# Where the second 1/rms of the feed-forward activations is multiplied in: inside the weight loop, or behind its last weight sum

## The chip, the cores and the metric

The kernel runs on one core of one Trainium2 chip. The metric is the device time in microseconds (us). The core has five engines that run their own queues of instructions in order: TensorE (PE; its weight loads are listed as PEld), VectorE (DVE), ScalarE (ACT), GpSimd (POOL) and SyncE (SP, which here only issues DMAs). Operands lie in SBUF; matmul results are written to PSUM, in eight banks of 128 x 512 float32.

## The reference

One layer of a decoder trunk on 512 tokens of width 1024, in float32: a mixer, a memory cross-attention and a feed-forward part, each with a residual. The change lies in the last:

```python
def rms_norm(x, g):
    var = jnp.mean(xf * xf, axis=-1, keepdims=True)
    return xf * lax.rsqrt(var + EPS) * g

hf = rms_norm(x, norm_ffn[l])
gate, up = jnp.split(hf @ w_ffn_in[l], 2, axis=-1)
x = x + (jax.nn.silu(gate) * up) @ w_ffn_out[l]
return rms_norm(x, norm_final)
```

FFN_HIDDEN is 2816, that is 22 tiles of 128. The 1/rms of a token is one factor for its whole row, so `hf @ w` can be computed without it and multiplied by it afterwards: once for the gate, ahead of silu, and once for `up`.

## The kernel before

Activations are held transposed: features on the 128 partitions, the 512 tokens along the free dimension. Each float32 operand is split into a rounded part (`hi`, a copy on ACT) and the rest (`lo`, a subtraction on VectorE), and each product is three matmuls (hi x hi, hi x lo, lo x hi).

The feed-forward input product is done by tiles m = 0 to 21, each with a gate and an up column block. For a tile the two column blocks, the two token halves and the pairs of feature blocks form a 2 x 2 block product, which is computed with seven products in place of eight. `product(m, i)` (i = 0 to 6, line 660) is 12 matmuls of 256 columns; the seven need seven combinations of the weights:

- `ffn_load(m)` (lines 619 to 629) fetches them: `wg` (two blocks), `ws` (one block to two places, line 625) and `a` from the SP queue, then a DMA from POOL's queue that adds two further blocks into `ws` (line 628). The tiles `wg` and `ws` share a ring of four buffers, as do later the rows of the output weights.
- `ffn_raw` (line 638) makes the two combinations that are still lacking, i = 3 and i = 6, by an addition on POOL: the weight sums.
- `ffn_form` splits each combination: the copy on ACT (L649), the subtraction on VectorE (L650). It runs six products ahead.

Results are put together from PSUM: `reads` (copies on ACT, L680; additions on VectorE, L682 and L685), `second` (VectorE, L690, which reads a bank that TensorE then goes on to accumulate in), and `evict` in three parts: part 0 multiplies the gate by 1/rms (`r2b`, a tile of 128 x 512 with the tokens' factors in every partition; VectorE, L697), part 1 is silu (ACT, L699), part 2 multiplies silu by `up` with the sign (VectorE, L704, two halves, one from PSUM and one from the SBUF tile `sb`) into `act[m]`, and then multiplies `act[m]` by `r2b` on POOL (L706).

The order of TensorE, ACT and VectorE in this part is written out by hand (`tc.manual_schedule`): the list `uses` interleaves the products of neighbouring tiles, and eviction of tile m-2 runs beside tile m. Tiles 20 and 21 are the last; their evictions come after the last products. POOL and SP are ordered by a scheduler.

The output product follows: `act[k]` is split (L169 on ACT, L170 on VectorE), the row block k of `w_ffn_out` is loaded and split (`load_w`, L143, L150, L151), and 8 x 3 matmuls of 512 columns (`out_step`, L155 to L157) add to eight PSUM banks that the input product used before. Tiles 0 and 1 are split inside the hand-written part, so that TensorE can start on the output product between the last input products. The last four row blocks are held back for `finish`, which adds the residual and makes the final norm.

Of the kernel before, what the change touches and what calls it, by code (L numbers as in the profile page):

```python
# [11 lines left out]
ALU = mybir.AluOpType  # L12
# [26 lines left out]
def hybrid_layer(ctx: ExitStack, tc: tile.TileContext, xT_d, memT_d, cols_d, wv_d, win_d,  # L39
                 wbr_d, wmix_d, wmq_d, wmk_d, wmv_d, wmo_d, wfi_d, wfo_d, out):  # L40
    nc = tc.nc
# [15 lines left out]
    def nm(s):  # L57
        count[0] += 1
        return f"{s}{count[0]}"

    def unit(s, cols=512):
        return upool.tile([P, cols], F32R, tag="u", name=nm(s), padded_shape=[P, 512])
# [4 lines left out]
    def f(ap):  # L67
        return ap.bitcast(F32)
# [38 lines left out]
    def after(i, earlier):  # L107
        for e in earlier:
            tc.add_manual_dep(i.ins, e.ins.name, mybir.DependencyInfo(
                mybir.DependencyClass.NoSync, mybir.DependencyReason.DATA), reason="order")  # L110
# [28 lines left out]
    def load_w(src, cols=P):  # L139

        k = D // cols
        raw = wpool.tile([P, D], F32, tag="wr", name=nm("wr"))
        i = nc.sync.dma_start(raw, src)  # L143
        if count[1] < FIRST:
            count[1] += 1
            chained(i)
        hi = wpool.tile([P, k, cols], F32R, tag="wh", name=nm("wh"))
        lo = wpool.tile([P, k, cols], F32R, tag="wl", name=nm("wl"))
        h2, l2 = (t.rearrange("p k c -> p (k c)") for t in (hi, lo))
        nc.scalar.copy(h2, raw)  # L150
        nc.vector.tensor_tensor(out=l2, in0=raw, in1=f(h2), op=ALU.subtract)  # L151
        return hi, lo
# [12 lines left out]
    def split(src, s, scale=None, cols=512):  # L165

        hi, lo = unit(s + "h", cols), unit(s + "l", cols)
        if scale is None:
            casts.append(nc.scalar.copy(hi, src))  # L169
            nc.vector.tensor_tensor(out=lo, in0=src, in1=f(hi), op=ALU.subtract)  # L170
        else:
            nc.scalar.activation(hi, src, AF.Copy, scale=scale)
            nc.vector.scalar_tensor_tensor(out=lo, in0=src, scalar=scale, in1=f(hi),
                                           op0=ALU.mult, op1=ALU.subtract)
        return hi, lo
# [260 lines left out]
    for m in range(KD):  # L436
# [8 lines left out]
        w = load_w(wbr_d[m])  # L445
# [11 lines left out]
    for m in range(KD):  # L457
        w = load_w(wmk_d[m])
# [11 lines left out]
    for n in range(2):  # L470
        pss = [ztile("vm") for _ in range(MT)]
        for c in range(4):
            w = load_w(wmv_d[n, c], 512)
# [82 lines left out]
    for h in range(MH):  # L556
# [12 lines left out]
        for t2 in range(2):  # L569
# [6 lines left out]
                                           in1=r1s[:, 2 * t2:2 * t2 + 2], op0=ALU.mult,  # L576
# [10 lines left out]
            for i in range(2):  # L587
                nc.vector.tensor_scalar(out=pr[:, i * MEM:(i + 1) * MEM],
                                        in0=pr[:, i * MEM:(i + 1) * MEM],
# [10 lines left out]
        for j in range(2):  # L600
# [3 lines left out]
            for m in range(MT):  # L604
                w = vm[m][c // 512]
# [5 lines left out]


    KP = KD // 2
    AHEAD = 6
    FORM_TAGS = ((wpool, "wh"), (wpool, "wl"), (wpool, "wh"), (wpool, "wl"), (fpool, "wf"))

    raws = {}

    def ffn_load(m):

        a = wfi_d[m].rearrange("p (i c) -> p i c", i=4)
        wg = wpool.tile([P, 2, 512], F32, tag="wr", name=nm("wg"))
        nc.sync.dma_start(wg, a[:, 0:2, :])
        s13 = wpool.tile([P, 2, 512], F32, tag="wr", name=nm("ws"))
        nc.sync.dma_start(s13, a[:, 2:3, :].broadcast_to([P, 2, 512]))
        a22 = fpool.tile([P, 512], F32, tag="w2", name=nm("a22"), bufs=4)
        nc.sync.dma_start(a22, a[:, 3, :])
        nc.gpsimd.dma_start(s13, a[:, 0:4:3, :], accum_op=ALU.add)  # L628
        raws[m] = [wg[:, 0, :], wg[:, 1, :], s13[:, 1, :], None, s13[:, 0, :], a22, None]

    def ffn_raw(m, i):
        if i == 0:
            ffn_load(m)
        w = raws[m]
        if w[i] is None:
            w[i] = fpool.tile([P, 512], F32, tag="w2", name=nm("s2"), bufs=4)
            a, b = (w[2], w[0]) if i == 3 else (w[3], w[1])
            nc.gpsimd.tensor_tensor(out=w[i], in0=a, in1=b, op=ALU.add)  # L638
        return w[i]

    wforms, made = {}, [0]
# [1 line left out]
    def ffn_form(m, i):  # L643

        raw = ffn_raw(m, i)
        pool, tag = FORM_TAGS[made[0] % len(FORM_TAGS)]
        made[0] += 1
        w = pool.tile([P, 2, 512], F32R, tag=tag, name=nm("wf"))
        nc.scalar.copy(w[:, 0, :], raw)  # L649
        nc.vector.tensor_tensor(out=w[:, 1, :], in0=raw, in1=f(w[:, 0, :]), op=ALU.subtract)  # L650
        wforms[m, i] = w

    def product(ps, m, i, ks=range(KP)):

        w = wforms[m, i]
        for k in ks:
            hi, lo = (w[:, j, k * P:(k + 1) * P] for j in range(2))
            xh, xl = x2f[k][i]
            for j, (a, b) in enumerate(((hi, xh), (hi, xl), (lo, xh))):
                nc.tensor.matmul(ps[:, :HS], a, b, start=i < 3 and k == 0 and j == 0,  # L660
                                 stop=k == KP - 1 and j == 2, skip_group_check=True)

    banks, act, silus, late = {}, {}, [], []
# [11 lines left out]
    def reads(m, i):  # L675

        b = banks[m]
        z, s, t = b["z"][:, :HS], b["s"], b["t"]
        if i in (0, 3, 4):
            nc.scalar.copy((s[:, :HS], None, None, s[:, HS:], t[:, :HS])[i], z)  # L680
        elif i == 1:
            nc.vector.tensor_tensor(out=b["g"][:, :HS], in0=b["v"][:, :HS], in1=s[:, :HS],  # L682
                                    op=ALU.add)
        elif i == 6:
            nc.vector.tensor_tensor(out=b["g"][:, HS:], in0=b["y"][:, :HS], in1=s[:, HS:],  # L685
                                    op=ALU.add)
# [6 lines left out]
    def evict(m, part):  # L693
        b = banks[m]
        g = b["g"]
        if part == 0:
            nc.vector.tensor_tensor(out=g, in0=g, in1=r2b[0], op=ALU.mult)  # L697
        elif part == 1:
            silus.append(nc.scalar.activation(g, g, AF.Silu))  # L699
        else:  # L700
            a = act[m] = f(unit("act"))
            for half, u in enumerate((b["z"][:, :HS], b["t"][:, HS:])):
                sl = slice(half * HS, (half + 1) * HS)
                nc.vector.scalar_tensor_tensor(out=a[:, sl], in0=u, scalar=-1.0, in1=g[:, sl],  # L704
                                               op0=ALU.mult, op1=ALU.mult)
            nc.gpsimd.tensor_tensor(out=a, in0=a, in1=r2b[0], op=ALU.mult)  # L706

    uses = [(0, 0), (0, 1), (0, 2)]
    for m in range(NF):
# [6 lines left out]
    r2b = [None]  # L716
    for n in range(AHEAD):
        ffn_form(*uses[n])
    with tc.manual_schedule(engines={mybir.EngineType.PE, mybir.EngineType.Activation,
                                     mybir.EngineType.DVE}):  # L720
        for ks in (range(KP - 1), range(KP - 1, KP)):
            for m, i in uses[:3]:
                product(bank_of(m, i) if ks[0] == 0 else banks[m]["zvy"[i]], m, i, ks)
        for n, (m, i) in enumerate(uses):
            if n > 2:
                product(bank_of(m, i), m, i)
            if (m, i) == (1, 0):
                r2b[0] = mean2[1]("r0b", bank=mmtile)
            if i == 4:
                reads(m, i)  # L730
            elif i == 5 and m == NF - 1:
                reads(m, i)
                second(m)
            else:
                if i == 1 and m > 0:
                    second(m - 1)
                reads(m, i)
            if n + AHEAD < len(uses):
                ffn_form(*uses[n + AHEAD])

            if i == 0 and m > 1:
                evict(m - 2, 0)
            elif i == 4 and 0 < m < NF - 1:
                evict(m - 1, 1)
            elif i == 1 and m > 1:
                evict(m - 2, 2)
            if m == NF - 1 and i in (0, 1):
                actp[i] = split(act[i], "act")
            if (m, i) == (NF - 2, 6):
                evict(m, 0)  # L750
                evict(m, 1)
            if (m, i) == (NF - 1, 5):
                evict(NF - 2, 2)
# [2 lines left out]
        evict(NF - 1, 2)  # L756
    r2b = r2b[0]
    act = [act[m] for m in range(NF)]


    acc = [mmtile("f") for _ in range(2)] + [ztile("f") for _ in range(4)]
# [7 lines left out]
    act = [actp[k] if k in actp else split(a, "act") for k, a in enumerate(act)]  # L769
    for k in range(NF - HOLD):  # L770
        w = load_w(wfo_d[k], D)
# [105 lines left out]
```

## Time and profile before

| | us |
|---|---|
| median of three runs | 895.28 |
| lowest and highest | 892.0, 899.22 |
| the profiled execution, its own time | 893.23 |
| the span in it, first to last instruction | 891.3 |

The profile is of one execution. Its times are measured from the start of the span. A row of the view in time has the start, the duration, the engine, the line, the operation, the output and the inputs, and in brackets how long the engine had been idle and what ended that. A row of the waits has the waiting engine and line, what it waited for, the sum, the number of waits and the longest. A row by stretches has the length, then for PE, PEld, DVE, ACT and POOL the busy time and the number of instructions, the granted TensorE clock, the share of DMA and GB/s. An engine's busy time includes what it spends inside an instruction that is held up. "wf<-ws" is output and inputs by the program's names.

The input product of the feed-forward part runs from 524.6 to 757.8 us, the output product from 754.8 to about 870.

### The profile page before, as it was taken

To read this page: it belongs to the slowest core of one execution; us is meant where nothing else is said; L and a number is where in the kernel's file an instruction comes from. 1 tells how busy PE (TensorE), PEld (TensorE's weight loads), DVE (VectorE), ACT (ScalarE), POOL (GpSimd) and SP (SyncE) were. 2 spreads that over 40 slices of the span, in tenths; PEclk is the share of its full clock that TensorE was granted. 3 is DMA by queue.
4 is the path that set the end of the run, shared out by engine and by line. 5 is a ranking of instruction groups with operands and counts; after the bars stand their busy time and mean duration, and the time that the engine had idled before them with its cause. 6 is when DMAs were issued, how large, how long until landed. Compare 5 with 4: busy or idle time off the path is not lost. (4 is left out here: it accounts for less than half of the span.)

```text
span 891.3 us, 12942 instructions
## 1 busy us (share of the span) xinstructions
PE 868.6 (97%) x5002; PEld 758.6 (85%) x5002; DVE 629.1 (71%) x951; ACT 438.6 (49%) x799; POOL 167.2 (19%) x177
## 2 busy tenths in 40 slices
PE   7999999999999999999999999999999998999995
PEld 5878887888888899888888889999999998888894
DVE  5768788886544566555555799999999998922236
ACT  5566576565332344433444565455555545711143
POOL 0021221111000000000000214555566543100003
PEclk9999999999999999999999999999999999999998
DMA  7332212225332345423211545667676665332202
GB/s 284 119 107 83 83 60 72 71 72 177 107 107 94 107 146 187 152 95 97 70 50 45 133 102 146 170 175 192 182 193 166 172 174 173 97 95 95 71 1 95
DMA packets 41469, 107.29 MB, mean 120 GB/s; under 512 B 3760, under 2 KB 7872, under 8 KB 41408
## 3 DMA queue, kind: packets, MB, share of 16 engines
q1 hardware_dynamic: 34848, 94.39, 31.8%
q0 software_dynamic: 6016, 11.56, 8.1%
q8 instruction: 39, 0.64, 0.3%
q10 hardware_dynamic: 544, 0.52, 0.2%
q14 instruction: 22, 0.18, 0.1%
HBM read 104.36 MB, written 2.10 MB: 119 GB/s over the span
## 5 line engine op out<-in xcount | busy, mean ns | idle before, releaser
L150 ACT CAST wh<-wr 128x1024 fp32r<-128x1024 f32 x106 | 111.3, 1052 | 246.7 <-issue 84.5
L151 DVE TENSOR_TENSOR wl<-wr,wh 128x1024 fp32r<-128x1024 f32 x106 | 130.1, 1227 | 100.1 <-ACT wh L150 99.8
L155 PE MATMUL pr<-xgh,wh 128*128 128x512 f32 x288 | 112.6, 391 | 0.1
L157 PE MATMUL pr<-xgh,wl 128*128 128x512 f32 x288 | 112.3, 390 | 0.0
L156 PE MATMUL pr<-xgl,wh 128*128 128x512 f32 x288 | 112.2, 390 | 0.0
L628 POOL DMA_DIRECT2D ws<-in_w_ffn_in_dram x22 | 26.4, 1202 | 320.7 <-DVE x L519 288.3
L155 PE MATMUL f<-acth,wh 128*128 128x512 f32 (+1 forms) x208 | 74.6, 359 | 0.3 <-DVE act L704 0.3
L156 PE MATMUL f<-actl,wh 128*128 128x512 f32 (+1 forms) x208 | 74.1, 357 | 0.0
L157 PE MATMUL f<-acth,wl 128*128 128x512 f32 (+1 forms) x208 | 74.1, 358 | 0.0
L660 PE MATMUL z<-xdh,wf 128*128 128x256 f32 x352 | 70.4, 283 | 0.0
L155 PEld LDWEIGHTS pr<-xgh,wh 128*128 128x128 f32 x288 | 54.1, 188 | 11.4 <-issue 0.4
L157 PEld LDWEIGHTS pr<-xgh,wl 128*128 128x128 f32 x288 | 54.1, 188 | 11.4
L156 PEld LDWEIGHTS pr<-xgl,wh 128*128 128x128 f32 x288 | 54.1, 188 | 10.7
L660 PEld LDWEIGHTS z<-xdh,wf 128*128 128x128 f32 x352 | 58.0, 192 | 0.0
L660 PE MATMUL z<-xdl,wf 128*128 128x256 f32 x176 | 49.8, 283 | 0.0
L638 POOL TENSOR_TENSOR s<-ws,wg 128x512 f32<-128x512 f32 x22 | 33.3, 1512 | 85.3 <-DMA ws<-in_w_ffn_in_dram 35.1
L650 DVE TENSOR_TENSOR wf<-ws,wf 128x512 fp32r<-128x512 f32 x44 | 45.5, 1033 | 3.5 <-ACT wf L649 3.5
L697 DVE TENSOR_TENSOR fg<-fg,r0b 128x512 f32<-128x512 f32 x22 | 46.3, 2103 | 0.0
L155 PEld LDWEIGHTS f<-acth,wh 128*128 128x128 f32 x208 | 39.3, 189 | 6.6 <-DVE act L704 0.7
L157 PEld LDWEIGHTS f<-acth,wl 128*128 128x128 f32 x208 | 39.1, 189 | 5.7
L156 PEld LDWEIGHTS f<-actl,wh 128*128 128x128 f32 x208 | 39.3, 189 | 5.5
L706 POOL TENSOR_TENSOR act<-act,r0b 128x512 f32<-128x512 f32 x22 | 38.3, 1742 | 13.9 <-DVE act L704 13.9
(256 smaller groups left out, 2291.6 us busy)
## 6 DMA issues: line engine op xcount, KB each, us to landing
wr<-in_w_in_dram SPq DMA_DIRECT2D x36, 512.0 KB, 3.4
wg<-in_w_ffn_in_dram SPq DMA_DIRECT2D x22, 512.0 KB, 4.9
ws<-in_w_ffn_in_dram SPq DMA_DIRECT2D x22, 512.0 KB, 4.8
ws<-in_w_ffn_in_dram POOLq DMA_DIRECT2D x22, 512.0 KB, 5.7
wr<-in_w_ffn_out_dram SPq DMA_DIRECT2D x22, 512.0 KB, 3.4
a<-in_w_ffn_in_dram SPq DMA_DIRECT2D x22, 256.0 KB, 3.3
wr<-in_w_branch_dram SPq DMA_DIRECT2D x8, 512.0 KB, 3.4
wr<-in_w_mem_k_dram SPq DMA_DIRECT2D x8, 512.0 KB, 3.4
```

Source lines behind the costliest of these rows:

```text
L150: nc.scalar.copy(h2, raw)
L151: nc.vector.tensor_tensor(out=l2, in0=raw, in1=f(h2), op=ALU.subtract)
L155: nc.tensor.matmul(ps, a[0], b[0], start=start, stop=False, **kw)
L156: nc.tensor.matmul(ps, a[0], b[1], start=False, stop=False, **kw)
L157: nc.tensor.matmul(ps, a[1], b[0], start=False, stop=stop, **kw)
L628: nc.gpsimd.dma_start(s13, a[:, 0:4:3, :], accum_op=ALU.add)
L638: nc.gpsimd.tensor_tensor(out=w[i], in0=a, in1=b, op=ALU.add)
L650: nc.vector.tensor_tensor(out=w[:, 1, :], in0=raw, in1=f(w[:, 0, :]), op=ALU.subtract)
L660: nc.tensor.matmul(ps[:, :HS], a, b, start=i < 3 and k == 0 and j == 0, stop=k == KP - 1 and j == 2, skip_group_check=True)
L697: nc.vector.tensor_tensor(out=g, in0=g, in1=r2b[0], op=ALU.mult)
L706: nc.gpsimd.tensor_tensor(out=a, in0=a, in1=r2b[0], op=ALU.mult)
```

## The change

For tiles 0, 1 and 2 the multiplication of `act[m]` by `r2b` on POOL stays where it was. For tiles 3 to 21 it is taken out of `evict` and issued after the hand-written part, still on POOL, and each is ordered behind the last weight sum (`after` adds an order without a semaphore).

```diff
+    SCALED = 3
...
-    raws = {}
+    raws, sums = {}, []
...
-            nc.gpsimd.tensor_tensor(out=w[i], in0=a, in1=b, op=ALU.add)
+            sums.append(nc.gpsimd.tensor_tensor(out=w[i], in0=a, in1=b, op=ALU.add))
...
-            nc.gpsimd.tensor_tensor(out=a, in0=a, in1=r2b[0], op=ALU.mult)
+            if m < SCALED:
+                nc.gpsimd.tensor_tensor(out=a, in0=a, in1=r2b[0], op=ALU.mult)
...
     act = [act[m] for m in range(NF)]
+    for a in act[SCALED:]:
+        after(nc.gpsimd.tensor_tensor(out=a, in0=a, in1=r2b, op=ALU.mult), sums[-1:])
```

In the built program the instructions of TensorE, VectorE, ACT and SP stand in the same order as before. On POOL the nineteen multiplications now follow one another behind the two last weight sums, in the order of the tiles; in the program before, tile m's stood behind the first weight sum of tile m+2 or so and ahead of the next DMA issue of POOL.

## The prediction

> **What bounds the kernel now.** First the head of the page and its row for the instruction that moves, then the busy time by stretches.
>
> ```profile
> span 891.3 us, 12942 instructions
> ...
> PE 868.6 (97%) x5002; PEld 758.6 (85%) x5002; DVE 629.1 (71%) x951; ACT 438.6 (49%) x799; POOL 167.2 (19%) x177
> ...
> L706 POOL TENSOR_TENSOR act<-act,r0b 128x512 f32<-128x512 f32 x22 | 38.3, 1742 | 13.9 <-DVE act L704 13.9
> ```
> ```profile
> 540.00:740.00 200.00, 197.68 (x1634) 195.63 (x1633) 195.06 (x252) 106.33 (x213) 107.37 (x76) 1.00 0.67 176
> ...
> 750.40:753.80 3.40, 3.40 (x18) 3.40 (x17) 2.52 (x5) 1.32 (x2) 0.00 (x0) 0.51 0.43 136
> ...
> 780.00:860.00 80.00, 80.00 (x373) 67.06 (x372) 19.97 (x20) 16.30 (x19) 0.00 (x0) 1.00 0.22 73
> ```
>
> TensorE is the bound nearly everywhere, so only time in which it stands still can be won. The columns of the second view are PE, PEld, DVE, ACT, POOL and then the granted clock. In the input half of the feed-forward part (540 to 740) VectorE is as full as TensorE, 195 of 200 us; in the output half (780 to 860) VectorE has 20 of 80 us and POOL nothing. The change carries POOL work from the full stretch to the empty one, but what counts is the passage between, 740 to 762. Third, who TensorE waits for from 515 to 765:
>
> ```profile
> PE z L660 <- ACT sa L680: 2.8, 2, 2.1
> PE y L660 <- DVE sb L690: 1.5, 5, 0.3
> PE f L155 <- DVE act L704: 0.3, 1, 0.3
> ```
>
> Fourth, one period of the loop, in time:
>
> ```profile
> 601.74 0.39 PE L660 MATMUL y<-xoh,wf 128*128 128x256 f32 x1 [0.32 <-DVE sb L690]
> ...
> 602.67 0.38 SPq L625 DMA_DIRECT2D ws<-in_w_ffn_in_dram  x1
> ...
> 603.67 1.40 POOL L638 TENSOR_TENSOR s<-ws,wg 128x512 f32<-128x512 f32 x1 [3.48 <-DMA ws<-in_w_ffn_in_dram]
> ...
> 603.83 1.78 DVE L650 TENSOR_TENSOR wf<-a,wf 128x512 fp32r<-128x512 f32 x1
> ...
> 605.03 1.76 POOL L706 TENSOR_TENSOR act<-act,r0b 128x512 f32<-128x512 f32 x1
> ...
> 605.54 0.41 DVE L685 TENSOR_TENSOR fg<-y,sa 128x256 f32<-128x256 f32 x1
> ...
> 605.87 1.46 DVE L650 TENSOR_TENSOR wf<-ws,wf 128x512 fp32r<-128x512 f32 x1
> ...
> 607.71 1.20 POOL L628 DMA_DIRECT2D ws<-in_w_ffn_in_dram  x1 [0.92 <-ACT wf L649]
> ...
> 608.46 2.35 DVE L697 TENSOR_TENSOR fg<-fg,r0b 128x512 f32<-128x512 f32 x1
> 608.48 1.76 POOL L638 TENSOR_TENSOR s<-s,wg 128x512 f32<-128x512 f32 x1
> ...
> 612.01 0.69 DVE L650 TENSOR_TENSOR wf<-ws,wf 128x512 fp32r<-128x512 f32 x1
> ...
> 612.73 0.38 SPq L625 DMA_DIRECT2D ws<-in_w_ffn_in_dram  x1
> ```
>
> A VectorE instruction with both inputs in SBUF takes 0.69 us alone (612.01) and 1.46 to 2.35 beside a POOL instruction, and it ends about 0.55 us after POOL's: 603.67+1.40 is 605.07 and the subtraction that began at 603.83 ends at 605.61; 605.03+1.76 is 606.79 and the next ends at 607.33. They take turns. The instruction at 605.54, which reads PSUM, takes its 0.41 us in the middle of a POOL instruction. So VectorE's full load is partly waiting, and each multiplication at L706 costs it 1.46-0.69 = 0.8 us a tile.
>
> **The change, part by part.** *The loop.* A row of twelve matmuls gives TensorE's pace:
>
> ```profile
> 727.06 1.60 PE L660 MATMUL z<-xf,wf 128*128 128x256 f32 x12
> 728.50 0.28 PE L660 MATMUL z<-xch,wf 128*128 128x256 f32 x1
> ```
>
> 1.44 us for twelve, 0.120 each; 1634 of them are 196.1 us of the 200, so 3.9 are lost. Of the two waits on ACT one lies past 740 (2.1), the other (2.8-2.1 = 0.7) before it; the loop itself loses 3.2. Those are the waits on DVE sb L690: VectorE comes late. With 16 multiplications gone from inside the loop (tiles 3 to 18) VectorE has 0.8 us more in each 10.06 us (602.67 to 612.73) and comes in time. What would be late next is the ring of the weight sum: plain DMA (602.67 to 607.71, 5.04), POOL's DMA issue and sum (to 610.25, 2.54), the blocked VectorE multiplication (to 610.81), three short ones and the subtraction (to 612.70) that frees the slot for the next plain DMA. It is as long as TensorE's 84 matmuls (84 x 0.120 = 10.1), and L706 is not in it: POOL idles 0.92 before its DMA issue. But a VectorE that comes 0.8 us earlier has L697 done ahead of POOL's sum, and the ring shortens by that. I take -3.0; the bounds are 0 (ring unchanged) and -3.9.
>
> *The passage.* The rows from the last tiles on, POOL first, then VectorE:
>
> ```profile
> 741.42 3.34 POOL L638 TENSOR_TENSOR s<-s,wg 128x512 f32<-128x512 f32 x2 [1.28 <-issue]
> ...
> 757.56 1.30 POOL L706 TENSOR_TENSOR act<-act,r0b 128x512 f32<-128x512 f32 x1 [7.42 <-DVE act L704]
> ```
> ```profile
> 741.81 1.78 DVE L697 TENSOR_TENSOR fg<-fg,r0b 128x512 f32<-128x512 f32 x1
> 743.52 1.79 DVE L170 TENSOR_TENSOR actl<-act,acth 128x512 fp32r<-128x512 f32 x1
> 745.23 0.68 DVE L650 TENSOR_TENSOR wf<-s,wf 128x512 fp32r<-128x512 f32 x1
> ...
> 747.77 1.21 DVE L151 TENSOR_TENSOR wl<-wr,wh 128x1024 fp32r<-128x1024 f32 x1
> 748.90 1.78 DVE L170 TENSOR_TENSOR actl<-act,acth 128x512 fp32r<-128x512 f32 x1
> ...
> 753.30 0.42 DVE L685 TENSOR_TENSOR fg<-y,sa 128x256 f32<-128x256 f32 x1 [0.88 <-PE y L660]
> ...
> 756.66 0.42 DVE L704 SCALAR_TENSOR_TENSOR act<-z,fg 128x256 f32<-128x256 f32 x1 [0.87 <-ACT fg L699]
> ...
> 757.82 0.42 DVE L685 TENSOR_TENSOR fg<-y,sa 128x256 f32<-128x256 f32 x1 [0.41 <-PE y L660]
> 758.16 1.77 DVE L151 TENSOR_TENSOR wl<-wr,wh 128x1024 fp32r<-128x1024 f32 x1
> ...
> 761.24 0.42 DVE L704 SCALAR_TENSOR_TENSOR act<-z,fg 128x256 f32<-128x256 f32 x1 [0.70 <-ACT fg L699]
> ```
>
> The last row is the eviction of tile 21, which hands TensorE its last PSUM bank; TensorE goes on at 761.7 and is not stopped after that. The chain of VectorE from 741.81 to there takes 19.4 us, in an order written out by hand that stays as it is. It holds four lock waits (1.78-0.68 three times, 1.77-1.21 once: 3.9) and 1.3 us of waiting for TensorE (0.88, 0.41); bare it is 14.2.
>
> After the change sixteen multiplications stand ready on POOL when the last sum (the second of 741.42) is issued, each holding VectorE off for about 1.25 us (1.30 at 757.56 alone). In the chain are twelve VectorE instructions with two SBUF inputs (three at L697, two at L170, three at L650, four at L151). Eight find POOL just begun, 1.25 each; four come behind one or two that read PSUM, 0.4 each, and wait 0.9, 0.9, 0.9 and 0.5: 10.0+3.2 = 13.2. The chain becomes 27.4 us. Bounds: 21, if each finds POOL half done (14.2 + 12 x 0.6), and 33, if the three L704 that read sb block as well (15 x 1.25). It starts earlier than at 741.81, since VectorE is no longer behind TensorE, which left tile 19's last product here:
>
> ```profile
> 735.67 0.28 PE L660 MATMUL z<-xdh,wf 128*128 128x256 f32 x1
> ```
>
> The product's result is there at 735.8; then VectorE has one PSUM read (0.34), three subtractions (0.60 each without the records' overlap) and one turn of POOL's sum (1.25), so the chain starts at 739.1 and ends at 766.5 in place of 761.24: +5.3 against an unchanged loop. This takes in TensorE's waits of 0.7, 2.1 and 0.3 us. The first two are for copies on ACT, which was held up by late weights:
>
> ```profile
> 737.04 0.62 ACT L649 CAST wf<-ws 128x512 fp32r<-128x512 f32 x1 [3.86 <-DMA ws<-in_w_ffn_in_dram]
> ...
> 746.50 1.04 ACT L150 CAST wh<-wr 128x1024 fp32r<-128x1024 f32 x1 [0.78 <-DMA wr<-in_w_ffn_out_dram]
> ```
>
> Those waits go when VectorE frees the weight slots earlier, but TensorE then waits for the evictions of tiles 20 and 21 instead, several us at a time.
>
> *The clock.* After the wait of 2.1 us the clock was 0.51 over 3.4 us (750.40), which is 1.7 us of work; in the trace VectorE's chain ended last anyway and hid part of it. After a wait of several us right before 766.5 nothing hides it: 0 to +1.7, I take +0.9.
>
> The Trainium skill ("TensorE: Matmul & The Clock Gate", Part 1: The HAM clock gate) says that the clock halves after an idle window of about 3.4 us. Here 2.1 us sufficed, so the measurement decides; by the page's rule the term would be 0 if the new waits stay below 3.4 us and +1.7 above, and the sum +2.3 or +4.0 where the rows give +3.2.
>
> *At nothing.* The splits of tiles 3 to 21 on ACT and VectorE now wait for POOL, and behind them stand the splits of the output weights. The first is needed when TensorE reaches tile 3, three tiles after 762 at 5.1 us each (80 us over 373 matmuls is 0.214, 24 a tile); POOL, one multiplication per 1.25+0.6, is done with nineteen 35 us after 740. Tile 7's weights, behind the last split, are wanted at about 798. Uncovered, one late split would cost what it is late. No DMA changes its queue; POOL's issues of the weight sum stand one multiplication less behind, and after the moved ones only the final scaling comes, 100 us later.
>
> Sum: -3.0 + 5.3 + 0.9 = **+3.2 us**. The profiled execution took 893.2 us (span 891.3); the runs' median is 895.3, so 898.5.
>
> **The rivals.**
> *Covered (0.15).* Multiplications fall into VectorE's pauses and the chain ends at 739.1+21 = 760, no longer behind TensorE, whose waits and clock come back too. The most is 3.2+0.7+2.1+0.3+1.7 = 8.0 us, 887.3; half of that is 891. For: VectorE needs 20 us in the 80 after 780. Against: not a pause over 0.9 us in the chain.
> *The ring holds (0.15).* Plain DMA, POOL and VectorE keep their 10.06 us; the loop wins nothing: +6.2, 901.5. For: SP issues ws every 10.06 us. Against: TensorE's waits name sb, not the forms.
> *Locked out (0.10), slower.* POOL goes from one ready multiplication to the next without a turn for VectorE: 16 x 1.25 = 20 us from 740, then the chain's remaining 13.6 bare: 773.6, +12.4, less 3.0, plus 0.9: 905.6. It decides at POOL's first two multiplications. Against: in the pair at 741.42 VectorE got its turn between (741.81 and 743.52 end 1.7 apart). The Trainium skill ("SBUF — State Buffer", Who interferes with whom) says that whoever issues first has the shared pair for the whole instruction and the other fully blocks; of turns it says nothing.
>
> **How the numbers follow.** The forecast has 0.60: +3.2, from the chain's bounds (21 and 33 for 27.4: -6 to +6) about -3 to +9, so 892 to 904. With the rivals, 889 to 906 leaves out the best of the covered case and the worst of the locked-out one, under 2 in 10. Over 1% (9 us; about what a measurement of this kernel can tell from no change) faster is more than even the whole 8.0 us, 0.04; slower by that is the locked-out case and the tops of the forecast and of the ring, 0.16; the rest is within.
>
> **What would show it.** Loop: the row 540 to 740 with over 1660 matmuls, no PE wait on sb; wrong if TensorE still waits there or SP's ws stays 10.06 apart with gaps. Passage: POOL in unbroken alternation from about 740 to 775, L650, L170 and L151 at 1.8 to 2.4 us, the last L704 about 26 us after the first L697 of the chain; TensorE waiting on DVE act and fg for 5 us or more in all. Locked out shows as one VectorE instruction over 5 us. If PE's waits in the passage are under 2 us, the forecast is wrong on the fast side.

## The result and the profile after

| | before | after |
|---|---|---|
| median of five runs, us | 895.28 | 901.10 |
| lowest and highest, us | 892.0, 899.22 | 899.26, 903.07 |
| profiled execution: its time, its span, us | 893.23, 891.3 | 899.26, 897.6 |

The ratio after to before is 1.0078, 95% interval 1.0053 to 1.0104: slower by 0.8%. The head of the page and the row of TensorE's and the others' busy time, then two stretches of the changed kernel, with the columns as before:

```profile
span 897.6 us, 12933 instructions
...
PE 869.2 (97%) x5002; PEld 759.6 (85%) x5002; DVE 624.5 (70%) x951; ACT 437.3 (49%) x799; POOL 168.5 (19%) x177
```
```profile
540.00:740.00 200.00, 198.56 (x1648) 197.48 (x1649) 181.56 (x256) 106.38 (x216) 81.28 (x61) 1.00 0.67 176
740.00:762.00 22.00, 13.10 (x95) 12.29 (x95) 21.05 (x19) 8.21 (x13) 21.92 (x13) 0.86 0.44 144
```

The loop did what was meant: POOL has 81 us of the 200 where it had 107, VectorE 182 where it had 195, and TensorE gets 14 more matmuls through. The passage pays for it: in the 22 us after 740 POOL is busy without a gap, VectorE nearly so, and TensorE does 95 matmuls, where it did 129 before. Whom it waited for from 515 to 770:

```profile
PE y L661 <- DVE sb L691: 7.3, 1, 7.3
PE z L661 <- ACT sa L681: 3.0, 3, 1.6
```

The five short waits on sb in the loop are gone; one of 7.3 us has come, in the passage. (Lines from 614 to 705 are one higher than before: L691 is `second`, L698 the multiplication of the gate, L705 the eviction into `act`, L762 the moved multiplications.) POOL, then VectorE, in time:

```profile
730.04 1.20 POOL L629 DMA_DIRECT2D ws<-in_w_ffn_in_dram  x1 [3.09 <-DVE fg L698]
735.78 1.29 POOL L639 TENSOR_TENSOR s<-ws,wg 128x512 f32<-128x512 f32 x1 [4.54 <-issue]
739.37 3.52 POOL L639 TENSOR_TENSOR s<-s,wg 128x512 f32<-128x512 f32 x2 [2.30 <-issue]
742.85 33.70 POOL L762 TENSOR_TENSOR act<-act,r0b 128x512 f32<-128x512 f32 x19
```
```profile
736.32 1.30 DVE L651 TENSOR_TENSOR wf<-ws,wf 128x512 fp32r<-128x512 f32 x1 [3.04 <-ACT wf L650]
...
739.94 1.79 DVE L698 TENSOR_TENSOR fg<-fg,r0b 128x512 f32<-128x512 f32 x1
741.65 1.79 DVE L170 TENSOR_TENSOR actl<-act,acth 128x512 fp32r<-128x512 f32 x1
743.36 1.78 DVE L651 TENSOR_TENSOR wf<-s,wf 128x512 fp32r<-128x512 f32 x1
...
745.73 1.10 DVE L651 TENSOR_TENSOR wf<-a,wf 128x512 fp32r<-128x512 f32 x1
...
747.09 1.16 DVE L705 SCALAR_TENSOR_TENSOR act<-sb,fg 128x256 f32<-128x256 f32 x1
748.17 2.31 DVE L151 TENSOR_TENSOR wl<-wr,wh 128x1024 fp32r<-128x1024 f32 x1
750.41 1.78 DVE L170 TENSOR_TENSOR actl<-act,acth 128x512 fp32r<-128x512 f32 x1
752.11 1.77 DVE L651 TENSOR_TENSOR wf<-s,wf 128x512 fp32r<-128x512 f32 x1
753.81 2.28 DVE L151 TENSOR_TENSOR wl<-wr,wh 128x1024 fp32r<-128x1024 f32 x1
...
756.35 1.95 DVE L151 TENSOR_TENSOR wl<-wr,wh 128x1024 fp32r<-128x1024 f32 x1
758.22 1.74 DVE L698 TENSOR_TENSOR fg<-fg,r0b 128x512 f32<-128x512 f32 x1
759.88 0.41 DVE L691 TENSOR_TENSOR sb<-y,sb 128x256 f32<-128x256 f32 x1
760.65 0.42 DVE L705 SCALAR_TENSOR_TENSOR act<-z,fg 128x256 f32<-128x256 f32 x1 [0.36 <-ACT fg L700]
...
763.32 0.42 DVE L686 TENSOR_TENSOR fg<-y,sa 128x256 f32<-128x256 f32 x1 [1.90 <-PE y L661]
763.66 1.22 DVE L151 TENSOR_TENSOR wl<-wr,wh 128x1024 fp32r<-128x1024 f32 x1
764.80 1.77 DVE L698 TENSOR_TENSOR fg<-fg,r0b 128x512 f32<-128x512 f32 x1
767.27 0.42 DVE L705 SCALAR_TENSOR_TENSOR act<-z,fg 128x256 f32<-128x256 f32 x1 [0.70 <-ACT fg L700]
```

Two sums and nineteen multiplications follow one another on POOL for 37 us, 1.77 each (33.70/19), where one alone takes 1.30. Beside them most VectorE instructions with two SBUF inputs last about 1.1 us longer than alone: fg 1.79 for 0.68, actl 1.79 for 0.68, wl 2.31 for 1.21. Those that read PSUM (L691, 0.41) keep their length. The sum for tile 21's sb stands behind most of them, at 759.88, and TensorE waits for it:

```profile
760.35 0.58 PE L661 MATMUL y<-xoh,wf 128*128 128x256 f32 x1 [7.27 <-DVE sb L691]
```

To compare runs, the span is cut at four rows that all have: the first matmul of the feed-forward input product, the first matmul of product (21, 0), the gate's multiplication of tile 19 (the chain's first instruction), and the first half of `act` of tile 21 (its last). Before: 524.64, 737.11, 741.81, 761.24, end 891.33. After: 525.38, 736.05, 739.94, 767.27, end 897.55. So the loop is 1.8 us shorter, the gap up to the chain 0.8 shorter, the chain 7.9 longer and what follows it 0.2 longer; the remaining 0.7 arose ahead of the feed-forward part, where nothing was changed. Together +6.2.

### The profile page after: what moved, and what is told of

It reads as the page before. It is cut to its first block, busy times and chain, and to the rows that moved or that the text cites. A ratio compares the mean times of both kernels' runs of the same rounds, so it can differ in the third digit from the quotient of the medians.

```text
span 897.6 us, 12933 instructions
## 1 busy us (share of the span) xinstructions
PE 869.2 (97%) x5002; PEld 759.6 (85%) x5002; DVE 624.5 (70%) x951; ACT 437.3 (49%) x799; POOL 168.5 (19%) x177
## 5 line engine op out<-in xcount | busy, mean ns | idle before, releaser
L151 DVE TENSOR_TENSOR wl<-wr,wh 128x1024 fp32r<-128x1024 f32 x106 | 133.6, 1261 | 95.9 <-ACT wh L150 95.7
L629 POOL DMA_DIRECT2D ws<-in_w_ffn_in_dram x22 | 26.4, 1200 | 343.0 <-DVE x L519 288.3
L650 ACT CAST wf<-ws 128x512 fp32r<-128x512 f32 x44 | 27.0, 615 | 51.1 <-DMA ws<-in_w_ffn_in_dram 51.1
L651 DVE TENSOR_TENSOR wf<-wg,wf 128x512 fp32r<-128x512 f32 x44 | 48.6, 1106 | 2.0 <-ACT wf L650 2.0
```

## The experiments

Where an edit is to the changed kernel, its ratio is still to the kernel before, run on the same chip. The table comes from the cuts just described; "start" is from product (21, 0) to the chain. The runs follow below it.

| run | median, us | ratio, 95% interval | loop | start | chain | after the chain | span |
|---|---|---|---|---|---|---|---|
| before | 895.28 | 1 | 212.5 | 4.7 | 19.4 | 130.1 | 891.3 |
| after | 901.10 | 1.0078, 1.0053 to 1.0104 | 210.7 | 3.9 | 27.3 | 130.3 | 897.6 |
| none | 893.67 | 0.998, 0.9957 to 1.0002 | 211.4 | 5.4 | 17.6 | 130.1 | 889.5 |
| late | 893.14 | 0.9993, 0.9973 to 1.0012 | 210.1 | 3.2 | 17.4 | 134.7 | 890.0 |
| sixteen spare | 901.53 | 1.0069, 1.005 to 1.0088 | 214.0 | 4.0 | 26.4 | 130.3 | 899.6 |
| sixteen memsets | 894.31 | 0.9998, 0.9981 to 1.0015 | 213.5 | 4.9 | 20.4 | 130.0 | 896.0 |
| halves | 897.08 | 1.0039, 1.0014 to 1.0063 | 215.7 | 5.1 | 23.0 | 131.0 | 902.3 |
| late, splits spread | 893.06 | 0.9986, 0.9963 to 1.001 | 211.4 | 3.9 | 17.3 | 130.1 | 887.9 |
| six spare | 902.82 | 1.0091, 1.0057 to 1.0125 | 214.9 | 4.7 | 24.1 | 131.8 | 901.2 |
| two in the loop | 906.05 | 1.0123, 1.0082 to 1.0165 | 221.7 | 5.4 | 21.7 | 130.4 | 904.6 |
| sb first | 900.49 | 1.0065, 1.0039 to 1.009 | 209.7 | 7.4 | 26.1 | 130.3 | 898.7 |

The median of before beside which they ran was 894.41 for none, late, sixteen spare and sixteen memsets, 894.1 for the next four, and 894.22 for sb first.

**None.** The nineteen moved multiplications are left out.

```diff
-    for a in act[SCALED:]:
-        after(nc.gpsimd.tensor_tensor(out=a, in0=a, in1=r2b, op=ALU.mult), sums[-1:])
```

> The multiplications of tiles 3 to 21 by 1/rms are left out altogether (the output lacks these factors); everything else as in the changed kernel. Turns theory (the added time is VectorE's instructions with two SBUF inputs being held off by POOL's multiplications in the passage, one each): without them the loop's gain stays and the passage is free, 889 to 892 us; VectorE's chain from tile 19's fg at L697 to tile 21's act takes 15 to 18 us. Rival (the loop itself or the weight ring became slower): 895 to 901, as in the changed kernel. Rival (the splits of the output half wait for the multiplications): also 889 to 892.

The chain falls to 17.6 us, below the 19.4 of before, and the span by 8.0 us. The chain alone is 9.7 us shorter than in the changed kernel, while the loop and the start took 2.2 us longer in this execution. So the multiplications behind the last sum cost what was lost, and they cost it in the chain. The median, 893.67, misses the 889 to 892 that were expected of the loop's gain: against before the interval holds 1.

**Late.** All nineteen are done, but tile 21's comes first on POOL. It needs `act` of tile 21, the last thing the chain makes, so POOL stays quiet until the chain has ended.

```diff
-    for a in act[SCALED:]:
-        after(nc.gpsimd.tensor_tensor(out=a, in0=a, in1=r2b, op=ALU.mult), sums[-1:])
+    for a in act[-1:] + act[SCALED:-1]:
+        sums.append(nc.gpsimd.tensor_tensor(out=a, in0=a, in1=r2b, op=ALU.mult))
+        after(sums[-1], sums[-2:-1])
```

> The multiplication of tile 21 goes first on POOL, then 3 to 20; as it waits for tile 21's eviction, none runs in the passage, all nineteen run beside the output half. Turns theory: loop's gain kept, passage free, 889 to 892, VectorE's splits in the output half at 1.8 us apiece but covered. Rival (splits wait for multiplications): these come 15 us later than in the changed kernel, so slower than it, 903 or more. Rival (loop or ring slower): 899 to 902.

The same work, some 14 us later, and the chain is 17.4 us and the median that of before (again not the 889 to 892 expected): what cost was not the multiplications as such, nor that the splits wait for them (they wait longer here), but that they met the chain. The splits did cost something of their own here. VectorE's rows of this run, then TensorE's and the stretch behind it:

```profile
772.59 12.03 DVE L170 TENSOR_TENSOR actl<-act,acth 128x512 fp32r<-128x512 f32 x7
784.55 2.28 DVE L151 TENSOR_TENSOR wl<-wr,wh 128x1024 fp32r<-128x1024 f32 x1
```
```profile
786.88 0.50 PE L157 MATMUL f<-acth,wl 128*128 128x512 f32 x1 [2.69 <-DVE wl L151]
```
```profile
788.00:791.80 3.80, 3.80 (x12) 2.93 (x11) 3.80 (x5) 2.71 (x5) 1.66 (x1) 0.55 0.37 125
```

The scheduler has put seven splits, each in turns with POOL, ahead of the next weight subtraction; TensorE runs out of weights for 2.7 us, and its clock is then 0.55 on average over 3.8 us. The part after the chain is 134.7 for 130.1.

**Sixteen spare multiplications.** The loop is that of before (SCALED is 19); behind the last sum come one memset and sixteen multiplications of a scratch tile, which nothing waits for, and then those of tiles 19 to 21.

```diff
-    SCALED = 3
+    SCALED = 19
...
+    for _ in range(16):
+        sums.append(nc.gpsimd.tensor_tensor(out=scr, in0=scr, in1=r2b, op=ALU.mult))
+        after(sums[-1], sums[-2:-1])
```

> The kernel before in its loop (tiles 0 to 18 multiplied where they were), but behind the last weight sum POOL has 16 multiplications of a spare tile by 1/rms, whose result nobody reads, and then those of tiles 19 to 21. Turns theory: the passage costs what it does in the changed kernel, without the loop's gain: 902 to 906, chain of about 27 us. Rival (splits wait): only tiles 19 to 21 are late, and they are used last: 895. Rival (loop or ring): 895.

901.53 us and a chain of 26.4: as slow as the changed kernel and just below the 902 to 906 expected, although no split of tiles 3 to 18 waits for POOL and the loop's program is that of before. The presence of POOL's work beside the chain is enough.

**Sixteen memsets.** The same, with `nc.gpsimd.memset(scr, 0.0)` in place of the sixteen multiplications.

> As the run with the 16 spare multiplications, but with 16 memsets of the same spare tile in their place: POOL is occupied and writes SBUF but reads nothing. If it is POOL's reading that VectorE takes turns with: no cost, 894 to 897, VectorE at 0.68 and 1.21 us beside the memsets. If any POOL instruction on SBUF holds VectorE off: 16 times a memset's time more in the chain, 900 to 906.

POOL and VectorE of this run:

```profile
749.05 9.27 POOL L765 MEMSET scr<- 128x512 f32 x16
```
```profile
751.54 1.21 DVE L151 TENSOR_TENSOR wl<-wr,wh 128x1024 fp32r<-128x1024 f32 x1
752.68 0.68 DVE L170 TENSOR_TENSOR actl<-act,acth 128x512 fp32r<-128x512 f32 x1
753.28 0.68 DVE L651 TENSOR_TENSOR wf<-s,wf 128x512 fp32r<-128x512 f32 x1
```

POOL is just as busy from 749.05 to 758.3, and VectorE's instructions take their bare 1.21 and 0.68. The time is that of before. So it isn't POOL's activity that holds VectorE off, but POOL's reading of SBUF. The Trainium skill ("SBUF — State Buffer", Who interferes with whom) says that a VectorE instruction with two SBUF inputs contends with a GpSimd instruction that reads SBUF, not with one that only writes it; these rows agree. A memset is short (0.58 us each), though, so this run alone doesn't part reading from length; the next one shows what length does.

**Halves.** The changed kernel with each moved multiplication as two instructions of 256 columns.

```diff
+        for c in range(2):
+            h = a[:, c * HS:(c + 1) * HS]
+            after(nc.gpsimd.tensor_tensor(out=h, in0=h, in1=r2b[:, c * HS:(c + 1) * HS],
+                                          op=ALU.mult), sums[-1:])
```

> The changed kernel with each of the nineteen moved multiplications issued as two of 256 columns: the same elements on POOL, 38 instructions of about 0.7 us in place of 19 of about 1.25. Turns theory: a VectorE instruction in the chain now waits for half as long, so the chain is some 6 us shorter than 27.3 and the time 895 to 897. Rival (what counts is the POOL work that lies in the passage): as the changed kernel, 900 to 902.

```profile
758.44 1.22 DVE L651 TENSOR_TENSOR wf<-s,wf 128x512 fp32r<-128x512 f32 x1
759.59 1.75 DVE L151 TENSOR_TENSOR wl<-wr,wh 128x1024 fp32r<-128x1024 f32 x1
```

Each VectorE instruction is now held 0.54 us (1.22 for 0.68, 1.75 for 1.21) in place of 1.1, the chain is 23.0, 4.3 shorter where some 6 were expected, and about half of the loss is gone (+3.0 us by the medians, where the change cost 5.8; the 897.08 lies at the upper end of the 895 to 897 expected). VectorE waits for one POOL instruction at a time, at either length: turns. And since a half (by estimate 1.30/2 = 0.65 us alone) is about as short as a memset and still holds VectorE, it is the reading that counts. In the profiled execution of this run the loop took 215.7 us, with TensorE waiting 4.2 us in it for copies into sa on ACT, which itself stood for late weights (up to 5.9 us before one copy); the program of the loop is that of the changed kernel, so this is a spread of the loop itself, to be remembered below.

**Late, splits spread.** As "late", with the splits and the weight rows of the output product in an order by hand, one of each in alternation.

```diff
-    act = [actp[k] if k in actp else split(a, "act") for k, a in enumerate(act)]
...
-    for k in range(NF - HOLD):
+    def row(k):
+        ready(k)
         w = load_w(wfo_d[k], D)
...
+    with tc.manual_schedule(engines={mybir.EngineType.Activation, mybir.EngineType.DVE}):
+        for k in range(4, NF - HOLD):
+            row(k)
```

> As the run with tile 21's multiplication first, and the splits of the output half are ordered by hand from row block 4 on: one split of an activation tile, then one of a weight block, in turn, where the scheduler had put six to seven activation splits before the next weight block. That run had lost a 2.7 us wait of TensorE for a weight split and a half-clock stretch after it, 4.4 us in all. Theory: these go, 888 to 890, faster than both kernels. Rival (nothing of the loop's gain is real, the profiles differ by chance): 893 to 895.

The part after the chain is back at 130.1, and the span of 887.9 is the shortest of all. The median, 893.06, is 0.1% below that of before, and the interval holds 1. That is not the 888 to 890 of the theory; it is where the rival put it (893 to 895), by which the shorter loops in the profiles are chance. So a gain from the loop is not shown by the time, and what the change was after is worth little here, if anything.

**Six spare multiplications.** As "sixteen spare", with six.

> As the run with 16 spare multiplications behind the last weight sum, with 6 of them. Turns theory: the first six of the chain's twelve instructions with two SBUF inputs wait, some of which waited for the sums before; half of the cost of 16, 897 to 899. Rival (the cost comes at once, as soon as POOL holds VectorE off and TensorE's clock halves): 900 to 902. Rival (small numbers are covered): 894 to 895.

POOL and TensorE of this run:

```profile
748.79 10.47 POOL L765 TENSOR_TENSOR scr<-scr,r0b 128x512 f32<-128x512 f32 x6
```
```profile
763.55 0.58 PE L661 MATMUL y<-xoh,wf 128*128 128x256 f32 x1 [3.76 <-DVE sb L691]
```

By the medians six cost as much as sixteen: 902.82, where the theory named 897 to 899 and the first rival 900 to 902. Part of that may be spread, since this profiled loop is 2.4 us longer than that of before with the same program. In the passage six cost most of what sixteen do: from the chain's start to the matmul that takes the last PSUM bank 26.2 us pass, with sixteen 27.3, before 19.9. The six are through at 759.26, all ahead of the sum that TensorE waits for; with the 3.76 us of waiting come 7 us at 0.51 of the clock (762.7 to 769.7), which reach past the chain's end: 131.8 for 130.1. The cost is not in proportion to the number of multiplications. That those ahead of the last sb decide fits this, but no run moves them alone.

**Two in the loop.** The kernel before, with a second multiplication into a scratch tile behind each tile's own.

```diff
             nc.gpsimd.tensor_tensor(out=a, in0=a, in1=r2b[0], op=ALU.mult)
+            nc.gpsimd.tensor_tensor(out=scr, in0=a, in1=r2b[0], op=ALU.mult)
...
+    scr = cpool.tile([P, S + 2], F32, tag="cu", name="scr", bufs=2)[:, :S]
```

> The kernel before with a second multiplication by 1/rms on POOL right behind each tile's own, into a spare tile that nobody reads: the loop's suspected cost doubled (and that behind tiles 19 to 21). Theory (each multiplication in the loop takes 0.8 us from a VectorE that is late, of which 0.15 us a tile reach TensorE): at least 3 us more, 897 to 901, TensorE waiting on DVE sb more than 1.5 us. Rival (POOL's multiplications in the loop cost TensorE nothing): 894 to 895.

```profile
540.00:740.00 200.00, 191.14 (x1562) 187.65 (x1562) 198.59 (x242) 101.79 (x203) 132.38 (x91) 1.00 0.65 170
```
```profile
PE y L660 <- DVE sb L690: 8.8, 17, 1.1
```

One more per tile costs the loop 9.2 us, and the time of 906.05 is beyond the 897 to 901 expected. TensorE waits on sb in nearly every period: VectorE, at 198.6 of 200 us, is now the bound. One fewer shortened the profiled loop by 1.8. So the price of a multiplication in the loop is not constant; it is far higher above the number that the kernel before has than below it.

**sb first.** The changed kernel, with `second(21)` ahead of tile 20's last sum and multiplication.

```diff
             if i == 4:
                 reads(m, i)
+                if m == NF - 1:
+                    second(m)
             elif i == 5 and m == NF - 1:
                 reads(m, i)
-                second(m)
```

> The changed kernel with one VectorE instruction put earlier: the sum that fills sb of tile 21, for which TensorE stood 7.3 us, comes ahead of tile 20's last fg and its multiplication instead of behind them; one weight subtraction slides ahead of tile 20's evictions in exchange. TensorE's wait then shrinks by the two instructions and the weight subtraction put behind, some 3.9 us (756.0 in place of 759.9). If that wait was what the end hung on, the passage is shorter by 3.9 us and by the half clock that follows it: about 896 us, ratio 1.002 to 1.004. If the end hung on VectorE's chain up to the eviction of tile 21, and TensorE's wait was only its longest symptom, TensorE gets through tile 21 earlier and then stands before the last bank instead; the chain loses at most its own wait of 1.9 us for TensorE: 26 us in place of 27.3, 899.5 to 901 us, ratio 1.006 to 1.008, and a new wait of TensorE on DVE act L706 of 4 us or more.

TensorE's three waits in this passage, then the end of VectorE's chain:

```profile
750.07 0.38 PE L661 MATMUL z<-xch,wf 128*128 128x256 f32 x1 [0.81 <-ACT sa L681]
758.78 0.58 PE L661 MATMUL y<-xoh,wf 128*128 128x256 f32 x1 [4.14 <-DVE sb L691]
768.84 0.50 PE L155 MATMUL f<-acth,wh 128*128 128x512 f32 x1 [0.82 <-DVE act L705]
```
```profile
764.44 0.41 DVE L705 SCALAR_TENSOR_TENSOR act<-z,fg 128x256 f32<-128x256 f32 x1
764.77 1.18 DVE L705 SCALAR_TENSOR_TENSOR act<-sb,fg 128x256 f32<-128x256 f32 x1
765.88 0.41 DVE L686 TENSOR_TENSOR fg<-y,sa 128x256 f32<-128x256 f32 x1
766.32 1.34 DVE L698 TENSOR_TENSOR fg<-fg,r0b 128x512 f32<-128x512 f32 x1
768.36 0.42 DVE L705 SCALAR_TENSOR_TENSOR act<-z,fg 128x256 f32<-128x256 f32 x1 [0.70 <-ACT fg L700]
```

The longest wait went from 7.3 to 4.1 us, and the time hardly moved: 900.49. The chain is 26.1, since VectorE no longer waits 1.9 us for TensorE, and TensorE has a new wait at its end, for the last bank. It is 0.8 us and not the 4 expected. One reason is that TensorE now has 21 matmuls of the output product between its wait on sb and that bank, in place of 16 (about 1.2 us). The other is that in the changed kernel it was late for the bank already. There the eviction that frees it ends at 767.69, and TensorE takes it with the second matmul of this row, at 768.09 (the one that waited for `act` at 761.7 in the kernel before):

```profile
767.86 0.62 PE L155 MATMUL f<-acth,wh 128*128 128x512 f32 x2
```

So in the changed kernel two paths end within 0.4 us of each other: VectorE's chain, and TensorE's wait on sb with the work at half clock behind it. With the second path shorter, the first alone ends the passage, and next to nothing is won. Both are long because VectorE is held: in "none" and "late", where POOL is quiet beside the chain, the chain is short and there is no such wait.

## Why the prediction was right, and where its steps were off

**The bound, and the place that decides.** Right. TensorE is full outside the passage, and the passage lasts at least as long as VectorE's chain up to tile 21's eviction: with the chain at 17.3 to 17.6 us (none, late, splits spread) the kernel can't be told from before, with 26 to 27 it is slower by 0.7 to 0.8%, and with sb first TensorE's wait was cut by 3 us with next to no effect. The chain is not all of it, which the prediction did not see: with six spare multiplications it is 24.1 and the loss 0.9%, and there TensorE takes the last bank 1.7 us after it is free, because of its wait on sb and the half clock.

**The length of the chain.** 27.4 us was forecast, 27.3 measured; two parts of it were off and nearly cancel, so that the agreement to a tenth is luck. The held rows, over their bare lengths, give 11.7 us of lock waits, not 13.2: a full turn costs 1.1, not 1.25, and one of those held (747.09, 1.16 for 0.42) is an eviction that reads sb, which the forecast had only in its upper bound, while one weight subtraction (763.66, 1.22) went through free. Then 1.9 us came that no step held, VectorE's wait at 763.32 for TensorE, which itself had started the product 7.3 us late and was running at half clock. 14.2 + 11.7 + 1.9, less 0.5 because one wait for silu fell from 0.87 to 0.36, is 27.3.

**The start of the chain.** This step failed. The chain was to start at 739.1 with an unchanged loop, since "VectorE is no longer behind TensorE", and the loop's gain of 3.0 was subtracted as well. It started at 739.94, in all 1.9 us earlier than before, where the two together said 5.7. What sets it is the DMA of the last weights, which the prediction had in its list of waits ("those waits go when VectorE frees the weight slots earlier") but not in the sum. SP's issue of the last `ws`, before and after, and before, POOL's DMA behind it and VectorE's wait for the copy of what it brings:

```profile
725.03 0.38 SPq L625 DMA_DIRECT2D ws<-in_w_ffn_in_dram  x1
...
731.41 1.21 POOL L628 DMA_DIRECT2D ws<-in_w_ffn_in_dram  x1 [2.28 <-ACT wf L649]
...
737.70 1.29 DVE L650 TENSOR_TENSOR wf<-ws,wf 128x512 fp32r<-128x512 f32 x1 [3.04 <-ACT wf L649]
```
```profile
723.94 0.38 SPq L626 DMA_DIRECT2D ws<-in_w_ffn_in_dram  x1
```

It comes 1.1 us earlier, POOL's DMA 1.4 earlier (730.04 for 731.41), and from there to the copy on ACT 5.63 us pass in both (735.67 and 737.04). VectorE stands 3.04 us for that copy after as before: it was not behind TensorE there but behind the weights, before the change too. TensorE's waits on ACT did not go either (3.0 us for 2.8). The slots were free earlier only by what the loop had won; the transfer itself is no shorter.

**The loop.** Mechanism right, size too large: the waits on sb vanished, and two in the loop brought more of them, but the stretch from 540 to 740 holds 1648 matmuls, not over 1660, so that by 0.120 each 2.2 us of the 3.9 lost are lost still. In spans the gain is 1.8 for 3.0. The prediction put 3.2 us of loss down to the waits on sb, whose row sums to 1.5. Even with 0.16 more for each of the five (a matmul's record, 0.28, outlasts the pace of 0.120) that is 2.3; where the rest of the 3.2 went it didn't ask. And TensorE's waits on ACT in this stretch grew from 0.7 to 1.3 us. The profiled loops with the multiplications inside took 212.5, 213.5, 214.0 and 214.9 us (before, sixteen memsets, sixteen spare, six spare), those without 209.7 to 211.4 in five runs and 215.7 in one. Each is one execution: a gain of some 2 to 3 us is likely in most, late weights can take all of it, and the medians do not show it (none, late and splits spread are 0.2% or less below before, and each interval holds 1).

**The clock.** Forecast +0.9 behind the chain, measured +0.2 there: for almost half of the time at half clock (0.51 from 755.6 to 766.0 by its stretch) TensorE stood still anyway, and what the rest cost lies in the 1.9 us inside the chain or beside the chain's last instructions. With six spare multiplications, where it came later, 1.7 us show behind the chain. The rule that the prediction cites from the Trainium skill ("TensorE: Matmul & The Clock Gate", Part 1: The HAM clock gate), an idle window of about 3.4 us, does not fit "late", where a wait of 2.69 us sufficed, nor the wait of 7.3 us, in which the clock was at half (from 755.7) 2.6 us after TensorE's last matmul had ended.

**TensorE's waits.** Forecast on the evictions of tiles 20 and 21, "several us at a time"; it was one wait of 7.3 us on `second` of tile 21, an instruction that stands among them, for a bank that must be read before the last product may go on. The amount was right and the name wrong. As sb first shows, this wait ends almost together with the chain, so that cutting it alone wins next to nothing.

**At nothing.** Right for the change: TensorE stands nowhere between 767 and the final norm, though the splits wait for POOL. The cover is thin, as "late" showed: there one late weight subtraction cost 4.6 us with the clock.

**The sum.** -3.0 + 5.3 + 0.9 = +3.2 was forecast for the profiled execution, +6.0 came (899.26 for 893.23; +5.8 by the medians), nearly twice as much. The chain's start put too early is 3.1 of it (736.1 forecast with the loop's gain, 739.94 - 0.74 = 739.2 measured), the clock -0.7, 0.7 arose before the feed-forward part, and what lies around the span was 0.2 less. The side and the range were right because the chain was long in the way that was forecast, by turns.

**The rivals.** The ring holds named 901.5, nearer to the 901.1 measured than the forecast's 898.5. It was half right: the loop did not stand quite still, with SP's issues of `ws` 10.14 us apart on average (541.37 to 723.94, 18 periods) for 10.25 before (540.61 to 725.03), but the weights did hold the chain's start. Covered fell: POOL's multiplications did not slip into pauses. Locked out fell: no VectorE instruction of the chain was held for more than about 1.1 us, which is less than one POOL multiplication.

## What to carry to other kernels

Work taken off a full stretch is paid where it lands: ask not how empty the engine is over the next 80 us, but what runs in the first 20 behind the point from which it is ready, and whether the two hold each other up. Here an order that lets POOL begin behind the last eviction in place of the last sum takes the whole loss away. And a chain's start has several releasers: before counting an engine as free earlier, follow the transfers it waits for, and don't count the same gain in the stretch and at its end.

## What the runs showed of the hardware

VectorE and POOL take turns over a long row, though not without exception: of the fourteen VectorE instructions with two SBUF inputs in the changed kernel's chain nine were held for about 1.1 us, three for 0.4 to 0.74, two not at all, and POOL's 1.30 grew to 1.77. An eviction of 128x256 that reads one PSUM and one SBUF operand kept its 0.41, and its twin with two SBUF operands behind it took 1.18 (764.44 and 764.77 of sb first). TensorE's clock was halved with waits of 2.06 us (before), 2.69 (late), 3.76 (six spare) and 7.27 (after), and not behind the one of 1.6 (after). By the mean clock of the stretches (0.51 over 3.4 us, 0.55 over 3.8, 0.51 over 7.0 and 0.51 over 10.4) half clock lasted 3.3, 3.4, 6.9 and 10.2 us: about one, one, two and three times 3.4. After the longest wait it went on for more than 5 us, though TensorE was at work again from 760.35. Why, no run here tells.
